# A hybrid decoder step on one Trainium2 core: x1 kept in the output and added by accumulating DMAs, the last tile's squares summed apart, and a GpSimd power in the first and the last norm

## The chip, the cores and the metric

The kernel runs on one core of one Trainium2 chip. The metric is the time of one execution on the device in microseconds (us), lower is better. The engines are TensorE (PE, with its weight loads as PEld), VectorE (DVE), ScalarE (ACT), GpSimd (POOL) and the DMA engines, whose transfers are issued here from the queue of SyncE (SP) and from that of GpSimd.

## What is computed

One layer of a hybrid decoder on 1024 prompt positions and 8 x 8 sample positions, 1088 columns in all, D = 1024, all in float32:

```python
h = rmsnorm(x, norm_mix_pre)
P = h @ w_in                      # ten blocks of 256 columns, for four mixers
mix = concat(conv(P), pool(P), hgrn2(P), conformer(P)) @ w_out
x = x + rmsnorm(mix, norm_mix_post)                     # "x1" below
h = rmsnorm(x, norm_ffn_pre)
ff = (silu(h @ w_gate) * (h @ w_up)) @ w_down           # hidden width 2816
x = x + rmsnorm(ff, norm_ffn_post)                      # yT, the output
# rmsnorm(x, g) = x * rsqrt(mean(x*x) + 1e-6) * g
```

The new states of the mixers are outputs too. Only `x1`, the two additions and the norms matter for the change.

## The kernel before

Features lie on the 128 partitions (eight tiles of 128 features), positions along the free dimension. Every product is made of three float32r products, of a high and a low part of each operand (`XH`, `XL`, `wop`), so each weight tile loaded from HBM is split by a cast on ScalarE and a subtraction on VectorE.

The work has four stages.

1. **Entry.** The rows of x come in position-major, nine tiles of 1024 features (`xs`), loaded from L204. For each of three chunks of positions (`CH`), `x_sq` (L214) squares the rows on ScalarE with a sum per row, `x_norm` (L222) makes the reciprocal root with `rsqrt_steps` (L102) and scales the rows, and `x_split` (L231) transposes them on TensorE and writes `XH` on ScalarE and `XL` on VectorE. `rsqrt_steps` is twelve small VectorE instructions: the mean plus epsilon, a first guess from the bits and the halved argument, and three Newton steps of three. The order on ScalarE, VectorE and TensorE is the one in which the code is written (the block from L240); GpSimd's and SyncE's is a scheduler's. Chunk 0 has two of the nine tiles.
2. **Mixers**, driven by hand-written queues of generators (`hook`, `fill`, L308 to L341).
3. **w_out, x1 and the gated product.** `residual` (L1142) adds the normed mix to x and stores the result, x1, in the HBM tensor `x1d` (L1155), half of the features for a piece of 272 positions at a time: eight stores. The gated products follow in Strassen form (L1388); their results go to HBM (`hd`, `hx`).
4. **w_down.** The first 16 hidden blocks are multiplied in Strassen form (L1616), into accumulators `acc[0..7]` (their tiles are called `t_...` and `acc`). The last six blocks are multiplied plainly by `down` (L1494, matmul at L1498), in three chunks of positions `DC` of 448, 384 and 256 columns. This last block of the program (L1729 to L1780) sets its own order on ScalarE, VectorE, TensorE and GpSimd. For each chunk c and each feature tile j it issues: the weight split of two tiles ahead (`ahead`), the load of x1 of this chunk if j is 0 (L1752 to L1756: four loads of two feature tiles), the products, the addition of the product to `acc[j]` on VectorE (L1761), the addition of the last square to the sum `sqa` (L1765), the square of `acc[j]` on ScalarE (L1767), for chunk 0 the additions of `add_p1` on GpSimd, and so many steps of the *previous* chunk's `finish` (L1770).

`finish` (L1713) closes a chunk: `stats` (L1077) sums `sqa` over the partitions with matmuls against a column of ones (L1082; a matmul on 128 positions stands twice in the counts of the trace), `rsqrt_steps` takes the root, `spread` transposes it over the partitions (L180), and for each of eight feature tiles VectorE scales `acc[j]` by gain and root (L1723), GpSimd (in the last chunk for j = 1, 4, 6, 7 VectorE) adds x1 (L1724), and SyncE stores the tile to `yT` (L1725). The chunks 0 and 1 are closed within the products of the chunks 1 and 2; the last chunk's closing stands alone at the end of the program. There the sum `sqa` takes the last square by one more addition on VectorE (L1773) ahead of `stats`.

SyncE's queue issues the loads of weights and the stores of `yT` in one order, and a store waits there for the addition that it stores.

## Time and profile before

| | |
|---|---|
| three runs | 1195.52 us median, 1193.73 to 1196.79 |
| the profiled execution | 1194.23 us, of which the span from the first to the last instruction is 1192.5 us |
| busy share of the span | PE 97%, DVE 75%, ACT 38%, POOL 8% |
| the chain that ended last | PE 85% of the span, DVE 5%, DMA 4% |
| DMA | 140.32 MB, mean 118 GB/s |

Busy times are averages over stages with different limits. PE is busy nearly all the time except at both ends of the program: the first matmul starts at 11.75 us, and after the last product, at 1175 us, only small matmuls follow. The view by stretches of time and the instructions in order of time show what each end waits for.

### The profile page before, as it was taken

To read this page: it belongs to the slowest core of one execution; us is meant where nothing else is said; L and a number is where in the kernel's file an instruction comes from. 1 tells how busy PE (TensorE), PEld (TensorE's weight loads), DVE (VectorE), ACT (ScalarE), POOL (GpSimd) and SP (SyncE) were. 2 spreads that over 40 slices of the span, in tenths; PEclk is the share of its full clock that TensorE was granted. 3 is DMA by queue.
4 is the path that set the end of the run, shared out by engine and by line. 5 is a ranking of instruction groups with operands and counts; after the bars stand their busy time and mean duration, and the time that the engine had idled before them with its cause. 6 is when DMAs were issued, how large, how long until landed. Compare 5 with 4: busy or idle time off the path is not lost.

```text
span 1192.5 us, 21885 instructions
## 1 busy us (share of the span) xinstructions
PE 1151.5 (97%) x8476; PEld 1116.0 (94%) x8476; DVE 892.2 (75%) x1853; ACT 456.3 (38%) x1006; POOL 100.4 (8%) x130
## 2 busy tenths in 40 slices
PE   5999999999999999999999999999999999999994
PEld 4899899998999999999999999999999999999994
DVE  6468979997675678777677787787676668887687
ACT  7534322253364453433333444344344442123321
POOL 1000000000000000000000000000001221036234
PEclk9999999999999999999999999999999999999997
DMA  8011112211155123031332453354364875654732
GB/s 261 29 43 24 36 37 68 41 36 36 33 161 169 39 74 129 23 103 69 105 103 83 159 168 113 127 176 146 98 196 130 280 261 168 239 165 126 258 109 89
DMA packets 105576, 140.32 MB, mean 118 GB/s; under 512 B 25152, under 2 KB 74432, under 8 KB 105472
## 3 DMA queue, kind: packets, MB, share of 16 engines
q1 hardware_dynamic: 99424, 115.52, 30.5%
q0 software_dynamic: 6048, 23.40, 5.6%
q8 instruction: 66, 1.08, 0.4%
q14 instruction: 38, 0.31, 0.1%
HBM read 98.31 MB, written 40.57 MB: 116 GB/s over the span
## 4 chain that ended last, share of the span: by engine, by line
PE 85%; DVE 5%; DMA 4%; issue 2%; ACT 2%; POOL 0%; SPq 0%; DVEq 0%; ACTq 0%; POOLq 0%
PE p L1388 27%; PE mm L984 18%; PE p L1616 13%; PE p L1116 8%; PE p L1297 6%; PE p L1498 4%; PE mm L139 2%; PE sm L798 2%; DMA hx<-hi 1%; DVE wop L65 1%; DMA hd<-hst 1%; DMA raw<-hx 1%; DVE xl L65 1%; DMA raw<-wgu 1%; PE p L1082 1%
## 5 line engine op out<-in xcount | busy, mean ns | idle before, releaser
L65 DVE TENSOR_TENSOR wop<-raw,wop 128x512 fp32r<-128x512 f32 (+2 forms) x296 | 197.9, 681 | 110.2 <-ACT wop L1007 100.3
L1007 ACT CAST wop<-raw 128x512 fp32r<-128x512 f32 (+1 forms) x240 | 142.5, 604 | 257.0 <-DVE raw L65 120.6
L1388 PE MATMUL p<-xh,wop 128*128 128x272 f32 x1216 | 235.3, 288 | 0.0
L1388 PEld LDWEIGHTS p<-xh,wop 128*128 128x128 f32 x1216 | 193.0, 188 | 0.0
L1388 PE MATMUL p<-t,wop 128*128 128x272 f32 x912 | 181.0, 290 | 5.7 <-DVE c L65 5.7
L984 PE MATMUL mm<-xh,wop 128*128 128x256 f32 (+2 forms) x864 | 176.8, 333 | 0.0
L1388 PE MATMUL p<-xl,wop 128*128 128x272 f32 x608 | 175.1, 288 | 0.0
L1388 PEld LDWEIGHTS p<-t,wop 128*128 128x128 f32 x912 | 147.3, 190 | 6.8 <-DVE c L65 6.8
L984 PEld LDWEIGHTS mm<-xh,wop 128*128 128x128 f32 x864 | 138.3, 188 | 6.2 <-issue 1.1
L1388 PE MATMUL p<-x,wop 128*128 128x272 f32 x456 | 132.5, 290 | 0.0
L1388 PEld LDWEIGHTS p<-xl,wop 128*128 128x128 f32 x608 | 114.3, 188 | 0.0
L1116 PE MATMUL p<-xh,wop 128*128 128x272 f32 x512 | 100.2, 292 | 2.0 <-DVE wop L65 2.0
L984 PE MATMUL mm<-xl,wop 128*128 128x256 f32 (+2 forms) x432 | 97.9, 335 | 0.0
L1388 PEld LDWEIGHTS p<-x,wop 128*128 128x128 f32 x456 | 86.5, 190 | 0.0
L1116 PEld LDWEIGHTS p<-xh,wop 128*128 128x128 f32 x512 | 82.1, 191 | 2.2 <-DVE wop L65 2.2
L1616 PE MATMUL p<-xh,wop 128*128 128x272 f32 x456 | 82.2, 289 | 1.1 <-ACT x L1627 1.1
L1616 PE MATMUL p<-xl,wop 128*128 128x272 f32 x456 | 81.4, 288 | 0.0
L71 DVE SCALAR_TENSOR_TENSOR y<-u,taps,y 128x1024 f32<-128x1024 f32 x60 | 77.0, 1284 | 1.6
L65 DVE TENSOR_TENSOR raw<-raw,raw 128x512 f32<-128x512 f32 (+1 forms) x123 | 71.3, 589 | 8.8 <-DMA raw<-wgu 7.3
L1116 PE MATMUL p<-xl,wop 128*128 128x272 f32 x256 | 74.3, 290 | 0.0
L1297 PE MATMUL p<-xh,wop 128*128 128x272 f32 x384 | 74.0, 289 | 0.0
L984 PEld LDWEIGHTS mm<-xl,wop 128*128 128x128 f32 x432 | 69.4, 188 | 3.4 <-issue 0.7
(332 smaller groups left out, 1988.1 us busy)
## 6 DMA issues: line engine op xcount, KB each, us to landing
raw<-wgu SPq DMA_DIRECT2D x88, 256.0 KB, 3.0
hx<-hi SPq DMA_DIRECT2D x84, 136.0 KB, 2.0
raw<-win SPq DMA_DIRECT2D x40, 256.0 KB, 3.0
hx<-x SPq DMA_DIRECT2D x64, 136.0 KB, 2.5
raw<-wdn SPq DMA_DIRECT2D x32, 256.0 KB, 3.7
xh<-hx POOLq DMA_DIRECT2D x15, 544.0 KB, 9.7
xl<-hx POOLq DMA_DIRECT2D x15, 544.0 KB, 10.5
x<-hx POOLq DMA_DIRECT2D x12, 544.0 KB, 9.3
```

What stands on the lines that cost most here:

```text
L65: (eng or V).tensor_tensor(out, a, b, op)
L71: (eng or V).scalar_tensor_tensor(out=out, in0=a, scalar=s, in1=b, op0=op0, op1=op1)
L139: PE.matmul(ps[c][:, :n], hl[:, wi, kk], X[k][:, o:o + n], start=k == 0 and wi == 0 and X is XH, stop=k == KT - 1 and wi == 1)
L798: PE.matmul(ps[:rows, g * P:(g + 1) * P], kk[:, o:o + rows], qz[hf][:, :, g * 64:(g + 1) * 64], start=True, stop=True, skip_group_check=True)
L984: PE.matmul(ps[c][:, :w], hl[:, wi, kk], X[k][:, o:o + w], start=k == order[0] and wi == 0 and X is XH, stop=k == order[-1] and wi == 1)
L1007: S.copy(hl[:, 0], raw)
L1082: PE.matmul(st[:, i:i + 1], sq[:, a:a + P], ones[:, :1], start=True, stop=True, skip_group_check=True)
L1116: PE.matmul(ps[nt][:, :PW], WO[nt][k // 4][:, wi, kk:kk + P], X[k][:, o:o + PW], start=k == korder[0] and wi == 0 and X is XH, stop=k == k ...
L1297: PE.matmul(ps[r][:, :PW], w[:, wi, (k % 4) * P:(k % 4 + 1) * P], X[k][:, o:o + PW], start=k == 0 and wi == 0 and X is XH, stop=k == KT - ...
L1388: PE.matmul(ps[:, :PW], wop[:, wi, kk * P:(kk + 1) * P], x(kk, xi), start=first and kk == 0 and wi == 0 and xi == 0, stop=kk == 3 and wi == 1,
L1498: PE.matmul(ps[:, :n], wd[:, wi, kk * P:(kk + 1) * P], hops[k][xi][:, o:o + n], start=first and kk == 0 and wi == 0 and xi == 0, stop=not ...
L1616: PE.matmul(ps[:, :PW], ws[name][wi][q], x[:, xi, pr], start=first and q == 0 and wi == 0 and xi == 0, stop=q == 1 and wi == 1, skip_group ...
```

## The change

- The HBM tensor `x1d` is gone. `residual` stores x1 in the output `yT` itself.
- In `finish` of chunk 0 and chunk 1, x1 is no longer loaded and added: after VectorE has scaled `acc[j]`, GpSimd's queue issues a DMA that adds the tile to what stands in `yT`. So eight loads of x1 (four of 448 KB, four of 384 KB), sixteen additions on GpSimd and sixteen stores from SyncE's queue go, and sixteen accumulating DMAs come. Chunk 2 still loads x1 (now from `yT`), adds and stores as before.
- In the last chunk the last square isn't added to `sqa`: `stats` runs on `sqa` without it, and a second `stats` adds the last square's sums in the same bank of PSUM.
- `rsqrt_pow` takes the place of `rsqrt_steps` in the first chunk's entry norm and in the last chunk's closing norm: the mean on VectorE, and one GpSimd instruction that raises it to the power -0.5.

```diff
+    mhalf = T(const, [P, 1], "mhalf")
+    V.memset(mhalf, -0.5)
...
+    def rsqrt_pow(src, shape, scale, tag):
+        m, y = T(const, shape, f"rs_{tag}m"), T(const, shape, f"rs_{tag}y")
+        TS(m, src, scale, EPS)
+        GP.tensor_tensor(y, m, mhalf[:, :1].to_broadcast(shape), ALU.pow)
+        return y
...
     def x_norm(c, ss):
-        for r in rsqrt_steps(ss[:, :len(idx)], [P, len(idx)], 1.0 / D, f"x{CH[c][1]}"):
-            yield
+        args = ss[:, :len(idx)], [P, len(idx)], 1.0 / D, f"x{CH[c][1]}"
+        if c == 0:
+            r = rsqrt_pow(*args)
+        else:
+            for r in rsqrt_steps(*args):
+                yield
...
-    def stats(sq, n):
+    def stats(sq, n, st=None, last=True):
-        st = bank()
+        first = st is None
+        if first:
+            st = bank()
-            PE.matmul(st[:, i:i + 1], sq[:, a:a + P], ones[:, :1], start=True, stop=True, skip_group_check=True)
+            PE.matmul(st[:, i:i + 1], sq[:, a:a + P], ones[:, :1], start=first and i == 0, stop=last, skip_group_check=True)
...
-    x1k = x1d.rearrange("(k p) t -> p k t", p=P)
+    x1k = yT.rearrange("(k p) t -> p k t", p=P)
...
-    def finish(c, sqa, x1t):
+    def finish(c, sqa, x1t, sq=None):
-        st, gr = stats(sqa, n)
-        for r in rsqrt_steps(st, [P, len(gr)], 1.0 / D, f"f{c}"):
+        st, gr = stats(sqa, n, last=sq is None)
+        if sq is not None:
             yield
+            stats(sq, n, st)
+        args = st[:, :len(gr)], [P, len(gr)], 1.0 / D, f"f{c}"
+        if x1t:
+            r = rsqrt_pow(*args)
+            yield
+        else:
+            for r in rsqrt_steps(*args):
+                yield
...
-            TT(y, y, x1t[j // 2][:, j % 2], ALU.add, eng=GP if c < 2 or j in (0, 2, 3, 5) else V)
-            SY.dma_start(yT[j * P:(j + 1) * P, o:o + n], y)
+            if x1t:
+                TT(y, y, x1t[j // 2][:, j % 2], ALU.add, eng=GP if j in (0, 2, 3, 5) else V)
+                SY.dma_start(yT[j * P:(j + 1) * P, o:o + n], y)
+            else:
+                GP.dma_start(yT[j * P:(j + 1) * P, o:o + n], y, accum_op=ALU.add)
...
-                for m in range(KT // 2):
+                for m in range(KT // 2 if c == 2 else 0):
...
             if j == KT - 1:
-                TT(sqa, sqa, sq, ALU.add)
-                prev, fin = fin, finish(c, sqa, x1[c])
-                if c == len(DC) - 1:
-                    next(fin)
+                if c < len(DC) - 1:
+                    TT(sqa, sqa, sq, ALU.add)
+                    prev, fin = fin, finish(c, sqa, x1[c])
+                else:
+                    prev, fin = fin, finish(c, sqa, x1[c], sq)
```

GpSimd's instructions at the end of the program, from the second half of chunk 1's closing to the last addition (`xl_...`, `xh_...` and `x_...` hold x1 there). Before:

```order
L65 TENSOR_TENSOR t_1_1352_10556<-t_1_1352_10556,xh_1685_13031 128x384
L65 TENSOR_TENSOR t_1_1353_10557<-t_1_1353_10557,xh_1685_13031 128x384
L65 TENSOR_TENSOR acc_1354_10558<-acc_1354_10558,xl_1686_13033 128x384
L65 TENSOR_TENSOR acc_1355_10559<-acc_1355_10559,xl_1686_13033 128x384
L65 TENSOR_TENSOR t_0_1348_10552<-t_0_1348_10552,xh_1717_13300 128x256
L65 TENSOR_TENSOR t_0_1350_10554<-t_0_1350_10554,xl_1718_13302 128x256
L65 TENSOR_TENSOR t_1_1351_10555<-t_1_1351_10555,xl_1718_13302 128x256
L65 TENSOR_TENSOR t_1_1353_10557<-t_1_1353_10557,x_13304 128x256
```

Now, the same place:

```order
L1751 DMA yT<-t_1_1351_10546 128x384
L1751 DMA yT<-t_1_1352_10547 128x384
L1751 DMA yT<-acc_1353_10548 128x384
L1751 DMA yT<-acc_1354_10549 128x384
L131 TENSOR_TENSOR rs_f2y_13519<-rs_f2m_13518,mhalf_78 128x2
L65 TENSOR_TENSOR t_0_1347_10542<-t_0_1347_10542,x_13266 128x256
L65 TENSOR_TENSOR t_0_1349_10544<-t_0_1349_10544,x_13268 128x256
L65 TENSOR_TENSOR t_1_1350_10545<-t_1_1350_10545,x_13268 128x256
L65 TENSOR_TENSOR t_1_1352_10547<-t_1_1352_10547,x_13270 128x256
```

The additions of chunk 1 have become DMA issues, and the power (L131) stands behind all of them and ahead of the last chunk's additions.

VectorE's instructions from the last product's addition to the first scaling of the last closing (`p_...` is a bank of PSUM, `xl_...` the sum of squares, `sq_...` a square, `rs_f2m` the mean). Before, the nine rows of the Newton steps cut after the first:

```order
L65 TENSOR_TENSOR acc_1355_10559<-p_13533,acc_1355_10559 128x256
L65 TENSOR_TENSOR xl_1635_12741<-xl_1635_12741,sq_12742 128x256
L65 TENSOR_TENSOR xl_1635_12741<-xl_1635_12741 128x256
L68 TENSOR_SCALAR rs_f2m_13559<-p_13556 128x2
L68 TENSOR_SCALAR rs_f2y_13561<-rs_f2m_13559 128x2
L68 TENSOR_SCALAR rs_f2h_13560<-rs_f2m_13559 128x2
L65 TENSOR_TENSOR rs_f2a_13562<-rs_f2y_13561 128x2
```

Now:

```order
L65 TENSOR_TENSOR acc_1354_10549<-p_13491,acc_1354_10549 128x256
L65 TENSOR_TENSOR xl_1634_12731<-xl_1634_12731,sq_12732 128x256
L68 TENSOR_SCALAR rs_f2m_13518<-p_13513 128x2
L71 SCALAR_TENSOR_TENSOR t_0_1347_10542<-t_0_1347_10542,prm_70,p_13522 128x256
L71 SCALAR_TENSOR_TENSOR t_0_1348_10543<-t_0_1348_10543,prm_70,p_13522 128x256
```

One addition and eleven small steps are gone between the product's addition and the first scaling; on TensorE the matmuls of L1082 for this chunk are four where they were two.

GpSimd's instructions at the start of the program (`y_...` is a row tile of x, `rs_...` a reciprocal root; the row ISA is a reload of a library of GpSimd's functions). Before:

```order
L454 MEMSET u_965 128x30
L454 MEMSET u_1678 128x30
L68 ISA
L68 TENSOR_SCALAR y_24_103<-y_24_103,rs_x384y_195 128x1024
L68 TENSOR_SCALAR y_27_106<-y_27_106,rs_x448y_279 128x1024
```

Now:

```order
L467 MEMSET u_955 128x30
L467 MEMSET u_1668 128x30
L131 ISA
L131 TENSOR_TENSOR rs_x256y_150<-rs_x256m_149,mhalf_78 128x2
L68 TENSOR_SCALAR y_25_105<-y_25_105,rs_x384y_185 128x1024
```

The reload keeps its place behind the last memset; the first instruction behind it is now the power of chunk 0's norm.

## Rows read from the trace of the kernel before

**Rows 1.** The page: TensorE's busy time, share of the span and instructions (its section 1), and the chain that ended last by engine (its section 4).

```profile
PE 1151.5 (97%) x8476; PEld 1116.0 (94%) x8476; DVE 892.2 (75%) x1853; ACT 456.3 (38%) x1006; POOL 100.4 (8%) x130
...
PE 85%; DVE 5%; DMA 4%; issue 2%; ACT 2%; POOL 0%; SPq 0%; DVEq 0%; ACTq 0%; POOLq 0%
```

**Rows 2.** Stretches of the program: from and to, length, then busy time (and instructions) of PE, PEld, DVE, ACT and POOL, granted clock, DMA share and GB/s. The first is everything from the end of the entry to the last chunk 0 product, the second chunk 1's products and chunk 2's first, the third a gap, the fourth chunk 2's other products, then the last norm, then the last closing.

```profile
41.00:1133.00 1092.00, 1082.48 (x8038) 1051.99 (x8036) 821.34 (x1674) 416.48 (x928) 69.31 (x95) 1.00 0.36 116
1133.00:1158.14 25.14, 25.14 (x153) 24.89 (x152) 20.41 (x41) 7.28 (x16) 10.59 (x8) 1.00 0.34 111
1158.14:1159.00 0.86, 0.05 (x1) 0.05 (x1) 0.76 (x3) 0.14 (x1) 0.00 (x0) 1.00 0.37 144
1159.00:1175.40 16.40, 16.34 (x135) 15.93 (x135) 14.27 (x36) 4.82 (x12) 6.53 (x6) 1.00 0.24 80
1175.40:1183.20 7.80, 1.70 (x6) 1.21 (x6) 5.53 (x18) 0.59 (x2) 2.61 (x3) 0.65 0.20 76
1183.20:1192.50 9.30, 0.00 (x0) 0.00 (x0) 5.91 (x12) 0.00 (x0) 2.85 (x4) 0.50 0.33 113
```

**Rows 3.** Instructions in order of time at the start: start, duration, engine, line, operation, output and inputs, and in brackets the idle time before it and what ended it.

```profile
4.07 0.18 POOL L454 MEMSET u<- 128x30 f32 x2
...
8.77 0.17 DVE L68 TENSOR_SCALAR rs_x256m<-ss 128x2 f32<-128x2 f32 x1 [4.30 <-ACT h L219]
...
10.94 1.42 DVE L68 TENSOR_SCALAR y<-y,rs_x256y 128x1024 f32<-128x1024 f32 x2
...
11.75 0.48 PE L236 MATMUL sm<-cst,y 128*128 128x128 f32 x1 [11.75 <-DVE y L68]
...
12.47 0.18 ACT L219 ACTIVATION_READ_ACCUMULATOR h<-y 128x1 f32 x1
...
12.92 0.47 ACT L237 ACTIVATE xh<-sm,prm 128x256 fp32r<-128x256 f32 x1 [0.27 <-PE sm L236]
...
18.80 1.60 POOL L68 TENSOR_SCALAR y<-y,rs_x384y 128x1024 f32<-128x1024 f32 x1 [14.55 <-DVE rs_x384y L71]
```

**Rows 4.** TensorE in order of time around the gap at 1158 us, columns as in rows 3, and the matmuls of chunk 1's spread.

```profile
1157.86 0.28 PE L1498 MATMUL p<-xl,wop 128*128 128x256 f32 x1
1158.95 0.83 PE L1082 MATMUL p<-ones,sq 128*128 128x1 f32 x6 [0.81 <-DVE sq L65]
...
1162.00 0.54 PE L180 MATMUL p<-cst,rs_f1y 128*128 128x128 f32 x3
```

**Rows 5.** VectorE in order of time ahead of that gap: the weight split, the addition of the last product of chunk 1, and the last two additions of squares.

```profile
1155.61 1.18 DVE L65 TENSOR_TENSOR wop<-raw,wop 128x384 fp32r<-128x384 f32 x1
1156.72 0.55 DVE L65 TENSOR_TENSOR acc<-p,acc 128x384 f32<-128x384 f32 x1
1157.19 1.71 DVE L65 TENSOR_TENSOR sq<-sq,xl 128x384 f32<-128x384 f32 x2
```

**Rows 6.** All engines in order of time from the last product to the last addition.

```profile
1174.99 1.17 DVE L65 TENSOR_TENSOR xl<-xl 128x256 f32<-128x256 f32 x1
1175.06 0.28 PE L1498 MATMUL p<-xl,wop 128*128 128x256 f32 x1
...
1176.09 1.12 DVE L71 SCALAR_TENSOR_TENSOR acc<-acc,prm,p 128x384 f32<-128x384 f32 x2
1176.82 2.12 POOL L65 TENSOR_TENSOR acc<-acc,xl 128x384 f32<-128x384 f32 x2 [0.94 <-POOL t L65]
1177.13 0.41 DVE L65 TENSOR_TENSOR acc<-p,acc 128x256 f32<-128x256 f32 x1
...
1177.64 0.42 ACT L1767 ACTIVATE xl<-acc 128x256 f32<-128x256 f32 x1 [2.06 <-DVE acc L65]
...
1178.20 1.03 DVE L65 TENSOR_TENSOR xl<-xl 128x256 f32<-128x256 f32 x1
...
1179.28 1.01 PE L1082 MATMUL p<-ones,xl 128*128 128x1 f32 x4 [3.94 <-DVE xl L65]
1180.33 0.16 DVE L68 TENSOR_SCALAR rs_f2m<-p 128x2 f32<-128x2 f32 x1 [1.10 <-PE p L1082]
...
1182.51 0.69 PE L180 MATMUL p<-cst,rs_f2y 128*128 128x128 f32 x2 [2.22 <-DVE rs_f2y L71]
1183.24 0.87 DVE L71 SCALAR_TENSOR_TENSOR t<-t,prm,p 128x256 f32<-128x256 f32 x2 [0.78 <-PE p L180]
```

**Rows 7.** VectorE's weight splits of 384 columns from 1119 to 1141.3 us, while GpSimd does nothing: count, busy time, mean ns of one.

```profile
L65 DVE TENSOR_TENSOR wop<-raw,wop 128x384 fp32r<-128x384 f32 x9 | 4.8, 556 | 3.4 <-ACT wop L1007 3.4
```

**Rows 8.** The same instruction from 1144 to 1159 us, while GpSimd adds x1.

```profile
L65 DVE TENSOR_TENSOR wop<-raw,wop 128x384 fp32r<-128x384 f32 x5 | 4.6, 917 | 0.0
```

**Rows 9.** Groups of GpSimd's instructions over the whole run: count, busy time, mean ns of one, idle time before them.

```profile
L1541 POOL DMA_DIRECT2D xh<-hx x15 | 8.1, 539 | 4.3 <-PE p L1616 1.6 <-DMA xl<-hx 1.4 <-DVE wop L65 0.5
...
L65 POOL TENSOR_TENSOR t<-t,x 128x256 f32<-128x256 f32 x1 | 0.7, 722 | 0.8 <-DVE t L71 0.8
...
L596 POOL MEMSET u<- 128x8 f32 x2 | 0.2, 118 | 0.0
```

**Rows 10.** Granted clock of TensorE after the last product (columns as in rows 2).

```profile
1176.40:1177.40 1.00, 0.00 (x0) 0.00 (x0) 1.00 (x3) 0.00 (x0) 0.58 (x1) 1.00 0.54 197
1177.40:1178.40 1.00, 0.00 (x0) 0.00 (x0) 0.90 (x3) 0.42 (x1) 1.00 (x2) 0.64 0.00 0
```

**Rows 11.** DMA issues by tile over the whole run: queue, count, KB each, median us from issue to landing.

```profile
xh<-hx POOLq DMA_DIRECT2D x15, 544.0 KB, 9.7
...
yT<-t SPq DMA_DIRECT2D x6, 224.0 KB, 1.9
```

More of the change, by code (lines that the diff above doesn't have):

```diff
@@ L53, in body @@
 def body(ctx, tc, xn, xT, win, wout, wgu, wdn, par, con, msk, poolw, s_conv, s_pool, s_hgrn, s_conf,
-         yT, o_conv_p, o_pool_p, o_hgrn_p, o_conf_p, o_conv_s, o_pool_s, o_hgrn_s, o_conf_s, x1d, hd, hx):
+         yT, o_conv_p, o_pool_p, o_hgrn_p, o_conf_p, o_conv_s, o_pool_s, o_hgrn_s, o_conf_s, hd, hx):
     nc = tc.nc
@@ L1076, in body @@
     LAG = 2
-    def stats(sq, n):
+    def stats(sq, n, st=None, last=True):
         gr = [min(a, n - P) for a in range(0, n, P)]
-        st = bank()
+        first = st is None
+        if first:
+            st = bank()
         for i, a in enumerate(gr):
-            PE.matmul(st[:, i:i + 1], sq[:, a:a + P], ones[:, :1], start=True, stop=True, skip_group_check=True)
-        return st[:, :len(gr)], gr
+            PE.matmul(st[:, i:i + 1], sq[:, a:a + P], ones[:, :1], start=first and i == 0, stop=last, skip_group_check=True)
+        return st, gr
     def spread(r, gr):
@@ L1133, in norm @@
         yield None
-        for r in rsqrt_steps(st, [P, len(gr)], 1.0 / D, tag):
+        for r in rsqrt_steps(st[:, :len(gr)], [P, len(gr)], 1.0 / D, tag):
             yield -0.2
@@ L1804 @@
          ("conf_p", (2, P, 30)), ("conv_s", (2, P, 8, 2)), ("pool_s", (2, P, 8, 15)), ("hgrn_s", (2, P, 8, 64)),
-         ("conf_s", (2, P, 8, 30)), ("x1", (D, NT)), ("hd", (NF, P, NT)), ("hx", (NPAIR, 7, P, 4 * PW))]
+         ("conf_s", (2, P, 8, 30)), ("hd", (NF, P, NT)), ("hx", (NPAIR, 7, P, 4 * PW))]
 def kernel(**inputs):
```

## The prediction

> **What bounds the kernel now.** I read the page first. TensorE is busy 97% of the span and carries 85% of the chain that ended last [rows 1], so only time in which TensorE stands still can be won without changing its work, and the change leaves its work alone. Next I read the busy times by stretches [rows 2]: from 41 to 1133 us TensorE is busy 1082 of 1092 us, and nothing that the change touches waits there but stores of x1, which go to another tensor of the same size. The change can act in three places only: the entry, until the first matmul at 11.75 us [rows 3]; a gap of 0.8 us at 1158 us, in front of chunk 1's sum of squares [rows 4]; and the end, where TensorE has finished its last product at 1175.3 us and the program goes on for 17 us. The instructions in order of time at these places show what each waits for.
>
> At the end [rows 6] the last matmul of a product starts at 1175.06 and takes 0.28 us. Its addition to `acc` on VectorE starts only at 1177.13, 1.8 us later, since VectorE is still at an addition of squares that took 1.17 us and at two scalings of chunk 1's closing. Then come the square on ScalarE (1177.64), the last addition of squares (1178.20, 1.03 us), the matmuls against ones (1179.28, 1.01 us), twelve small VectorE steps (1180.33 to 1182.5), the spread (0.69 us) and the first scaling at 1183.24. From the end of the product to that scaling it is 7.9 us, and the last closing takes the other 9.3 us [rows 2].
>
> Why VectorE is late is seen by comparing one instruction in two stretches: the weight split of 384 columns takes 556 ns while GpSimd is idle [rows 7] and 917 ns on the mean while GpSimd adds x1 [rows 8]. VectorE and GpSimd hold each other up.
>
> **The change part by part.**
>
> *Chunk 0 and 1: additions become DMAs.* Sixteen GpSimd additions of over 1 us each go; each is replaced by a DMA issue from GpSimd's queue, 539 ns by the issues that it has already [rows 9]. The freed time on GpSimd is worth nothing itself. What counts is that VectorE works at its undisturbed speed. Ahead of the gap the split took 1.18 us, and the last two additions of squares 1.71 us together [rows 5]; undisturbed, the addition to `acc` for the last product of chunk 1, which ends at 1156.0, starts there instead of at 1156.72, and the last sum is ready by about 1157.8. TensorE wants it when chunk 2's first product is through, at 1158.14, so the gap closes: **0.8 us**, and no less than 0.4 if half the disturbance stays.
>
> The same holds in chunk 2. A step with two scalings has a split of 0.5, an addition of 0.35, one of squares of 0.35 and 1.1 us for the scalings, 2.3 us, against TensorE's 2.1 us for a step (16.4 us for seven products and 1.2 of small matmuls [rows 2, 4]; the first of the eight is ahead of the gap). VectorE falls behind by a few tenths in two steps, and the step with a single scaling and the later ones without a split give it back. I count VectorE as idle when the last product ends.
>
> SyncE's queue loses the stores that waited for GpSimd, so weight loads come no later than before. Eight loads of x1 go too; TensorE waited for none, and that is worth nothing. GpSimd's queue gets a new order: the last power stands behind the sixteen DMA issues. The last two scalings of chunk 1 end before the last product does, so two issues of 0.54 us are over before the mean is ready. This cover is gone if the issue takes several times as long.
>
> *The last sum.* Counted from the end of the last product, 1175.34, on the old clock: the addition 0.06 later and 0.41 long, 1175.8; the square on ScalarE 0.1 later and 0.42 long, 1176.3. Meanwhile VectorE adds the square before it (0.42 undisturbed), and TensorE's first four matmuls run from 1176.2. Eight of them are due. Before, six took 0.83 us at chunk 1's end [rows 4] and four took 1.01 us at the end [rows 6]; by then the granted clock had fallen to its lower level, from 1.00 at 1177.4 to 0.5 [rows 10], 2.3 us after the products ended. In the changed order the pause is 0.9 us, so I take the faster row: 1.1 us, to 1177.3. At the lower clock it would be 2.0.
>
> *The power.* The mean, 0.16 us and a step between engines of 0.04 to 0.1 on each side: 1177.6. GpSimd's power of 128x2 has no row. Below, it can't be faster than the memset of eight columns, 0.12 us [rows 9]; above, I take the 1.6 us of the 128x1024 scaling [rows 3], though a power is more than a product per element and could exceed that. The nearest row is the smallest addition with two inputs, 128x256 in 0.72 us [rows 9], and two columns are far fewer: I take 0.4 us. Then 1178.0. The spread takes 0.36 at the full clock (two of the three that took 0.54 [rows 4]), and the first scaling starts at 1178.45 instead of 1183.24: **4.8 us**, between 2.5 (power 1.6, lower clock) and 5.1.
>
> *The last closing* has the same instructions: eight scalings, four additions on each engine, eight stores. Nothing.
>
> *The entry.* The power replaces the steps from 8.94 to 10.94 us [rows 3]: with 0.4 us and the steps between engines the rows are scaled from 9.5 us on, 1.4 us earlier, and so is the first matmul. But ScalarE's `xh`, which the first product needs, stood at 12.92 us with a wait of only 0.27 us; ahead of it ScalarE squares the rows of chunk 1, until 12.65 [rows 3]. So 0.27 us is won there, and more only where TensorE's earlier start makes it quicker behind that. **0.3 us**, between -0.5 (power at 2 us) and 1.4.
>
> Here a rule speaks against it. GpSimd's queue holds a library reload between its last memset, which ends at 4.25, and its first computing instruction, which starts at 18.80 [rows 3]. The trace shows no record of it, only that 14.5 us were enough. Before, nothing wanted GpSimd until 18.6; now the power does at 9.0. If the reload were over by 9.0, the term is 0.3. The Trainium skill (GPSIMD Engine Reference, 2.1 Instruction dispatch) says that the first call of freshly loaded code costs about 6 us; by that the power starts at about 10.2, an estimate from that page, the rows are scaled near the old time, the term is 0.1 and the sum 5.7. No run so far shows it.
>
> **Sum.** 0.3 + 0.8 + 4.8 = 5.9 us. The profiled execution took 1194.23 us, 1.3 below the median of 1195.52; taken off the median, that gives **1189.6 us**.
>
> **The rivals.**
>
> *The power is slow, or VectorE stays disturbed.* GpSimd now writes descriptors instead of adding, and that may hold VectorE too; a power of 2 to 3 us makes the closing term 2 to 3 and the entry -0.5 to -1.2. For it: the power has no row. Against it: GpSimd's 539 ns issues are short. It gives 2 to 3.5 us, 1192 to 1193.5.
>
> *The reload ends late.* If it lasts nearly until GpSimd's first instruction did, 18.8 us, the rows are scaled 8 us later, and all behind shifts: 5.6 won, 8 lost, 1198. It decides from a reload that ends after 15 us. Against it: the rows would not show a first scaling by GpSimd at 18.80 that follows VectorE's last step so closely unless the reload was done before.
>
> *The accumulating DMAs set the end.* This one ends slower. A plain store of 224 KB lands 1.9 us after its issue [rows 11]. An accumulation reads and writes; if it took 3.8 us and one could only follow another, sixteen of them from 1142 us on would end at 1203 us, 10.5 us behind the old end: 1206. It decides from 3.2 us each (50 us for sixteen). If they overlap, the last, issued near 1174, has 12 us until the new end at 1186.6, more than the 9.7 us that GpSimd's DMAs of 544 KB take in their bursts [rows 11]. For it: nothing in the trace accumulates. Against it: that queue's DMAs overlap, and these are smaller.
>
> *It doesn't do what it says.* The additions go for certain, by the order of instructions; but VectorE could be late at the last product for its own work alone (scalings and squares), 2.3 against 2.1 us a step. Then 1 to 1.5 us of the closing's 4.8 stay: 1191.
>
> **How the numbers follow.** A difference of 0.3% (3.6 us) is about what a measurement of this kernel can tell from none. The forecast has 55%; with the last rival, still mostly faster, 12%; more than 7 us won because the entry gains its whole 1.4 us, 6%; the slow power or disturbance 15%, nearly all of it within 0.3%; the late reload 7%, within 0.3% or beyond; the accumulations 5%. So faster 0.74, same 0.19, slower 0.07. The range takes the forecast's bounds: 8.0 us won at best gives 1187.5, less half a microsecond for the median's scatter, 1187.0; 2.5 us won gives 1193.0. Outside lie the two rivals of the other side and some of the slow power.
>
> **What would show it.** Right: no TensorE gap in front of chunk 1's sum of squares; VectorE's split at 0.56 us throughout; the last addition to `acc` within 0.2 us of the last product; under 4 us from the last product to the first scaling; the power near 0.4 us. Wrong: GpSimd's first power far behind the first mean; issues of accumulating DMAs well over 0.54 us, or their landing after the last store; TensorE's last small matmuls at the lower clock. If the power takes over 2 us, or the program ends on an accumulation, the forecast is wrong.

## The result, and the profile after

| | before | changed |
|---|---|---|
| first comparison, median (lowest to highest) | 1194.62 us (1192.17 to 1196.79) | 1181.66 us (1180.14 to 1182.58) |
| ratio, 95% interval | | 0.9893, 0.9868 to 0.9919 |
| second comparison (e1 below) | 1194.88 us | 1187.30 us, 0.9929, 0.9906 to 0.9953 |
| profiled execution, span | 1192.5 us | 1180.8 us |

The direction was as forecast, the size was not: 5.9 us were predicted, the first comparison gave 13.0 and the second 7.6. The page of the changed kernel, its head and the chain that ended last (they answer to [rows 1]):

```profile
span 1180.8 us, 21827 instructions
...
PE 1145.0 (97%) x8480; PEld 1111.1 (94%) x8480; DVE 881.4 (75%) x1831; ACT 455.5 (39%) x1006; POOL 96.8 (8%) x132
...
PE 84%; DVE 5%; DMA 4%; issue 2%; ACT 2%; POOL 1%; SPq 0%; DVEq 0%; ACTq 0%; POOLq 0%
```

TensorE's busy time is the first surprise. It has four instructions more than before by this count (the second set of sums at the end is two matmuls, and each stands twice) and is busy 6.5 us less.

The entry in order of time (the answer to [rows 3]):

```profile
8.58 0.17 DVE L68 TENSOR_SCALAR rs_x256m<-ss 128x2 f32<-128x2 f32 x1 [4.56 <-ACT h L228]
...
8.83 0.71 POOL L131 TENSOR_TENSOR rs_x256y<-rs_x256m,mhalf 128x2 f32<-128x2 f32 x1 [4.55 <-DVE rs_x256m L68]
9.57 1.42 DVE L68 TENSOR_SCALAR y<-y,rs_x256y 128x1024 f32<-128x1024 f32 x2 [0.82 <-POOL rs_x256y L131]
...
10.38 0.47 PE L249 MATMUL sm<-cst,y 128*128 128x128 f32 x1 [10.38 <-DVE y L68]
...
12.48 0.46 ACT L250 ACTIVATE xh<-sm,prm 128x256 fp32r<-128x256 f32 x1
...
12.99 0.58 PE L148 MATMUL mm<-xh,wop 128*128 128x256 f32 x1 [0.61 <-ACT xh L250]
```

The power starts 0.08 us behind the mean and takes 0.71. From the mean to the first matmul it is 1.80 us instead of 2.98. But ScalarE's `xh` is hardly earlier, and from the mean to the 151st matmul, at 41 us, it is 32.3 us against 32.6.

The gap of [rows 4] in front of chunk 1's sum of squares is closed; VectorE has the sum ready before TensorE is through with the product:

```profile
1150.09 0.56 DVE L65 TENSOR_TENSOR sq<-sq,xl 128x384 f32<-128x384 f32 x1 [0.19 <-ACT xl L1793]
...
1150.56 0.28 PE L1513 MATMUL p<-xl,wop 128*128 128x256 f32 x1
...
1150.71 0.83 PE L1097 MATMUL p<-ones,sq 128*128 128x1 f32 x6
```

The end, from the last product on (to be laid beside [rows 6]):

```profile
1166.59 0.28 PE L1513 MATMUL p<-xl,wop 128*128 128x256 f32 x1
1166.67 1.73 POOL L1751 DMA_DIRECT2D yT<-acc  x2 [1.06 <-DVE acc L71]
1166.90 0.43 DVE L65 TENSOR_TENSOR acc<-p,acc 128x256 f32<-128x256 f32 x1 [0.23 <-PE p L1513]
1167.24 0.42 DVE L65 TENSOR_TENSOR xl<-xl,sq 128x256 f32<-128x256 f32 x1
1167.42 0.42 ACT L1793 ACTIVATE xl<-acc 128x256 f32<-128x256 f32 x1 [1.62 <-DVE acc L65]
1167.72 1.05 PE L1097 MATMUL p<-ones,xl 128*128 128x1 f32 x8 [0.85 <-DVE xl L65]
1168.81 0.16 DVE L68 TENSOR_SCALAR rs_f2m<-p 128x2 f32<-128x2 f32 x1 [1.15 <-PE p L1097]
1169.05 0.72 POOL L131 TENSOR_TENSOR rs_f2y<-rs_f2m,mhalf 128x2 f32<-128x2 f32 x1 [0.65 <-DVE rs_f2m L68]
1169.82 0.43 PE L189 MATMUL p<-cst,rs_f2y 128*128 128x128 f32 x2 [1.06 <-POOL rs_f2y L131]
1170.30 0.87 DVE L71 SCALAR_TENSOR_TENSOR t<-t,prm,p 128x256 f32<-128x256 f32 x2 [1.33 <-PE p L189]
```

The last product's end is 1166.87. The addition to `acc` follows 0.03 us later (before, 1.8), and the first scaling 3.43 us later (before, 7.90). VectorE's weight split is undisturbed through both closings, and GpSimd's queue pays more for an issue than before (VectorE's group from 1130 to 1168 us, GpSimd's two groups over the whole run; [rows 7 to 9]):

```profile
L65 DVE TENSOR_TENSOR wop<-raw,wop 128x384 fp32r<-128x384 f32 x12 | 6.7, 555 | 2.0 <-ACT wop L1020 2.0
```

```profile
L1751 POOL DMA_DIRECT2D yT<-t x12 | 10.4, 948 | 46.9 <-DVE t L71 46.4 <-issue 0.5
L1751 POOL DMA_DIRECT2D yT<-acc x4 | 3.5, 1024 | 3.3 <-issue 2.3 <-DVE acc L71 1.1
```

An accumulation of 224 KB lands 5.2 us after its issue, by the list of DMA issues; the plain store took 1.9 [rows 11].

Where did 11.7 us of span go? Matmuls of the two traces were paired in order, and the distances from one matmul's start to the next one's compared. After 41 us some 8,280 of these distances differ by less than 20 ns; their differences add up to **-5.3 us**. The larger ones add up to -2.6: the gap (-0.9) and one fall of TensorE's clock less than before (-1.7), while the waits for VectorE elsewhere cancel out. The closing gives -4.5, the entry and its loads -0.5. And the stretch from the first scaling to the end of the span is *longer*: 10.52 us against 9.22, though from the first scaling to VectorE's last addition it is 6.05 us in both.

### The profile page after: what moved, and what is told of

Its sections match the earlier page's. It is cut to its first block, busy times and chain, and to the rows that moved or that the text cites. A ratio compares the mean times of both kernels' runs of the same rounds, so it can differ in the third digit from the quotient of the medians.

```text
span 1180.8 us, 21827 instructions
## 1 busy us (share of the span) xinstructions
PE 1145.0 (97%) x8480; PEld 1111.1 (94%) x8480; DVE 881.4 (75%) x1831; ACT 455.5 (39%) x1006; POOL 96.8 (8%) x132
## 4 chain that ended last, share of the span: by engine, by line
PE 84%; DVE 5%; DMA 4%; issue 2%; ACT 2%; POOL 1%; SPq 0%; DVEq 0%; ACTq 0%; POOLq 0%
PE p L1403 27%; PE mm L997 16%; PE p L1631 14%; PE p L1131 8%; PE p L1513 6%; PE p L1312 5%; PE mm L148 2%; PE sm L811 1%; DVE wop L65 1%; DMA raw<-wgu 1%; DMA hx<-hi 1%; DVE raw L65 1%; DMA y<-xn 1%; DMA raw<-hx 1%; PE sm L886 1%
## 5 line engine op out<-in xcount | busy, mean ns | idle before, releaser
L1403 PE MATMUL p<-xh,wop 128*128 128x272 f32 x1216 | 235.1, 288 | 0.0
L1403 PEld LDWEIGHTS p<-xh,wop 128*128 128x128 f32 x1216 | 193.3, 188 | 0.0
L1403 PE MATMUL p<-t,wop 128*128 128x272 f32 x912 | 179.3, 288 | 5.2 <-DVE c L65 5.2
L1403 PE MATMUL p<-xl,wop 128*128 128x272 f32 x608 | 175.6, 289 | 0.0
L997 PE MATMUL mm<-xh,wop 128*128 128x256 f32 (+2 forms) x864 | 175.3, 331 | 0.0
L1403 PEld LDWEIGHTS p<-t,wop 128*128 128x128 f32 x912 | 145.6, 188 | 6.5 <-DVE c L65 6.5
L997 PEld LDWEIGHTS mm<-xh,wop 128*128 128x128 f32 x864 | 137.4, 188 | 6.0 <-issue 1.1
L1403 PE MATMUL p<-x,wop 128*128 128x272 f32 x456 | 131.0, 287 | 0.0
L1403 PEld LDWEIGHTS p<-xl,wop 128*128 128x128 f32 x608 | 114.4, 188 | 0.0
L997 PE MATMUL mm<-xl,wop 128*128 128x256 f32 (+2 forms) x432 | 97.3, 333 | 0.0
L1403 PEld LDWEIGHTS p<-x,wop 128*128 128x128 f32 x456 | 86.0, 189 | 0.0
L1631 PE MATMUL p<-xh,wop 128*128 128x272 f32 x456 | 81.6, 287 | 1.1 <-ACT x L1642 1.1
L1631 PE MATMUL p<-xl,wop 128*128 128x272 f32 x456 | 81.0, 287 | 0.0
L997 PEld LDWEIGHTS mm<-xl,wop 128*128 128x128 f32 x432 | 69.2, 188 | 3.3 <-issue 0.8
```

Of the source, the lines that this page charges most:

```text
L997: PE.matmul(ps[c][:, :w], hl[:, wi, kk], X[k][:, o:o + w], start=k == order[0] and wi == 0 and X is XH, stop=k == order[-1] and wi == 1)
L1403: PE.matmul(ps[:, :PW], wop[:, wi, kk * P:(kk + 1) * P], x(kk, xi), start=first and kk == 0 and wi == 0 and xi == 0, stop=kk == 3 and wi == 1,
L1631: PE.matmul(ps[:, :PW], ws[name][wi][q], x[:, xi, pr], start=first and q == 0 and wi == 0 and xi == 0, stop=q == 1 and wi == 1, skip_group ...
```

## Experiments

Three things were not in the prediction: the shorter matmuls in a stretch that the change doesn't edit, the longer last stretch, and an entry that gained nothing. The theory for the first: the change makes the pool `const` smaller by 96 bytes (four small tiles less for the root, one more for the exponent, of 32 bytes each). `const` and the pools of `xh`, `xl` and `x` are allocated from the same side of SBUF, so all these tiles lie 96 bytes higher. In the built programs the first xh tile stands at byte 156000 of a partition before and at 156096 after; weights and PSUM places of all matmuls in L997, L1403 and L1631 are the same. Rival: chance between executions. Of e6 and e8 to e12 below there is one execution each; they are read by their rows, not by their times.

**e1: the changed kernel again.**

> The changed kernel once more, unaltered, as the yardstick for the next three on the same chip. Between 41 and 1133 us, where the change edits nothing, its profiled execution was 6 to 7 us shorter than that of the kernel before. Theory A (addresses): `const` shrank by 96 bytes, so every tile allocated on the same side (xh, xl, x) moved from an address 32 past a multiple of 64 to a multiple of 64, and matmuls that read them are about 1% shorter; a fixed property of the build. Theory B (scatter): the two profiled executions differ by chance in that stretch. A: ratio to the kernel before 0.989 again, matmuls of L1631 in 930 to 1095 us every 124.5 ns again. B: ratio nearer 0.995, and these spacings anywhere between 124.5 and 125.6.

1187.30 us (six runs, 1181.13 to 1191.86), 0.9929. The spacings came again to 0.05 ns (L997 on xh 165.7, L1631 on xh 124.4), so they belong to the build. The runs scatter for another reason: the profiled one, 1190.1 us of span, has four falls of the clock to 1.2 GHz between 300 and 960 us where the first profile has one. In the stretch with the first of them TensorE was busy all the time in both profiles, yet the clock was granted differently (busy times by stretch, columns as in [rows 2]; of e1, then of the first profile of the same kernel):

```profile
300.00:320.00 20.00, 20.00 (x109) 17.67 (x108) 10.76 (x39) 3.89 (x6) 0.00 (x0) 0.83 0.17 40
```

```profile
300.00:320.00 20.00, 20.00 (x131) 17.96 (x130) 12.71 (x43) 5.83 (x10) 0.00 (x0) 1.00 0.16 40
```

22 matmuls less in 20 us. The other three falls come behind waits of TensorE. In the 7.4 us ahead of the one at 901.4 us it was busy for 4.45 us; in the first profile it stood still there nearly as long, and the clock stayed (e1, then the first profile):

```profile
894.00:901.40 7.40, 4.45 (x36) 4.23 (x34) 6.54 (x13) 4.42 (x9) 0.00 (x0) 1.00 0.34 106
```

```profile
894.00:901.40 7.40, 4.84 (x39) 4.69 (x38) 6.79 (x16) 1.76 (x3) 0.00 (x0) 1.00 0.50 159
```

Before the last closing, e1's profile has 13.7 us more at 1.2 GHz. Half of that, 6.8 us, is an estimate of what it costs, of the 9.3 us by which its span is longer; another 1.2 us is its first mean, which comes at 9.82 us instead of 8.58. The mean granted clock of the first comparison's four runs was 0.993 to 0.996, that of these six 0.989 to 0.994. So the clock helped the 13.0 us and hurt the 7.6; whether by chance alone or by the chip on which they ran, no run here separates.

**e2 and e3: an unused tile of 32 bytes in `const`**, in the changed kernel and in the kernel before.

```diff
+    T(const, [P, 8], "pad")
```

> The changed kernel with an unused tile of 32 bytes in `const`, so that xh, xl and x lie 32 past a multiple of 64 again. A: 3 to 5 us slower than the changed kernel on this chip, matmuls on x, xh and xl in 41 to 340 us and 930 to 1095 us 1 to 2 ns longer each. B: within 1 us of it.

> The kernel before with the same unused tile of 32 bytes, so that xh, xl and x lie at multiples of 64; nothing else differs. A: 3 to 5 us faster than the kernel before (about 1190). B: the same time (ratio 1.000, within 0.1%).

e2: 1188.85 us, 1.5 slower than e1, less than expected and within the scatter of e1's runs. e3: 1192.69 us, 0.9981 of the kernel before (0.9966 to 0.9996), 2.2 us faster: an unused tile alone changes the time. But the multiple of 64 is not the rule: e3's matmuls on xh in L985 (L997 in the changed kernel) fell from 167.7 to 166.7 ns, those of 930 to 1095 us stayed at 125.6, where e2's also were. The theory was right on addresses and wrong on which.

**e4: the kernel before again.**

> The kernel before, unaltered, for a second profile of it. A: spacings of L1616's matmuls 125.6 ns as in the first profile. B: they differ from the first profile by as much as the changed kernel's did (1 ns). The wait of 1.85 us at 705 us and the fall of the clock at 901 us, which only the first profile of the kernel before has, come again if they belong to it, and not if they are chance.

1193.80 us, 0.9992. All spacings as in its first profile (167.7, 125.6). Two matmuls at 705 us that start 1.85 us apart in the first profile start 0.60 us apart here, so that wait is chance. The fall of the clock at 901 us is not: it came again, at 898 us. The 17 profiles of both kernels and their variants have their falls at the same places of the program, at 305 to 309 us in 9 of them, at 337 to 342 us in 10, at 895 to 903 us in 15. The changed kernel's first profile is one of the two without the last; e1, the same kernel, has it. So the 1.7 us of one fall less above are the luck of that execution.

**e5: the kernel before at the changed kernel's addresses.**

```diff
-            return T(const, shape, f"rs_{tag}{i}", dt)
+            return T(const, [P, 4], f"rs_{tag}{i}", dt)[:, :shape[1]] if tag == "f" else T(const, shape, f"rs_{tag}{i}", dt)
...
-        for r in rsqrt_steps(st, [P, len(gr)], 1.0 / D, f"f{c}"):
+        for r in rsqrt_steps(st, [P, len(gr)], 1.0 / D, "f"):
...
+    T(const, [P, 40], "pad")
```

> The kernel before with const smaller by 96 bytes (the three closings' small tiles share buffers, and an unused tile of 160 bytes fills up), so that xh, xl and x lie at exactly the changed kernel's addresses; nothing else of the change. Absolute address as the cause: matmuls of 41 to 340 us on xh 165.7 ns apart (kernel before 167.7), those of 930 to 1095 us 124.4 (125.6), and 3.5 to 5 us faster than the kernel before. Rival, another part of the build (the x1 tensor that is gone, the number of instructions): spacings as with the tile of 32 bytes, 166.7 and 125.6, and 2 us faster at most.

1190.61 us against 1194.33, 0.9973 (0.9955 to 0.9991): 3.7 us for nothing but addresses. Paired with the first profile of the kernel before, its small differences add up to -5.3 us, the same as the changed kernel's; e4, the kernel before against itself, gives +0.2. One view shows it: matmuls of the Strassen w_down product in 130 us without a gap (busy times by stretch, of that line alone: PE and its count, PEld and its count, granted clock, DMA share, GB/s). Before, changed, e5:

```profile
950.00:1080.00 130.00, 130.00 (x1038) 130.00 (x1037) 1.00 0.60 202
```

```profile
950.00:1080.00 130.00, 130.00 (x1047) 130.00 (x1046) 1.00 0.61 204
```

```profile
950.00:1080.00 130.00, 130.00 (x1047) 130.00 (x1046) 1.00 0.61 203
```

**e13: the whole change at the old addresses.**

```diff
+    T(const, [P, 24], "pad")
```

> The whole change, with an unused tile of 96 bytes in const, so that xh, xl and x lie at the addresses of the kernel before. If address and edits are the whole of the gain: the end and the gap as in the changed kernel, matmuls of 930 to 1095 us 125.6 ns apart as in the kernel before, and 4.1 us (2.5 to 5.5) faster than the kernel before. Rival, the edits also act in the middle of the program in a way not found yet: 7 us or more.

1189.36 us against 1194.61, 0.9967 (0.9953 to 0.9982): 3.9 us by the ratio, 5.3 by the two medians. The same view:

```profile
950.00:1080.00 130.00, 130.00 (x1037) 130.00 (x1037) 1.00 0.60 201
```

Its closing takes 3.43 us, the last stretch 10.52, as in the changed kernel. So the edits are worth 4 to 5 us and the addresses about as much: 3.7 by e5's medians, 5.3 by the paired traces.

**e7 and e8: the additions back on GpSimd**, for both chunks (e7, whose edit follows) and for chunk 1 alone (e8, with `c in (1, 2)` in the first line).

```diff
-                for m in range(KT // 2 if c == 2 else 0):
+                for m in range(KT // 2 if c in (0, 1, 2) else 0):
...
-        if x1t:
+        if c == 2:
             r = rsqrt_pow(*args)
...
-                TT(y, y, x1t[j // 2][:, j % 2], ALU.add, eng=GP if j in (0, 2, 3, 5) else V)
+                TT(y, y, x1t[j // 2][:, j % 2], ALU.add, eng=GP if c < 2 or j in (0, 2, 3, 5) else V)
```

> The changed kernel with chunk 0's and 1's additions on GpSimd and plain stores again (x1 still kept in yT, loaded from there). GpSimd's additions delay VectorE: the gap ahead of chunk 1's sum of squares is back at 0.8 to 1.1 us, and from the last product's end to the first scaling it is 4.5 to 5.2 us instead of 3.4. Rival, VectorE is late for its own work: gap and 3.4 us stay as in the changed kernel. GpSimd's last drain, which ended 1.2 us behind everything else in the changed kernel: it is 3.5 us long from GpSimd's last addition, as before, with 42 DMAs on its queue instead of 58. In all 1 to 2 us slower than the changed kernel.

> The changed kernel with only chunk 0 by accumulating DMAs, chunk 1 by GpSimd additions and plain stores. GpSimd's queue then has 50 DMAs, the last accumulation over long before the end. If its closing drain takes a fixed time for each DMA that its queue had (3.53 us for 42, 4.83 for 58, so 83 ns each), it is 4.2 us. If it waits for late accumulations, it is 3.5. The gap ahead of chunk 1's sum of squares stays closed, as chunk 0's closing runs under chunk 1's products; the last stretch is like that of the kernel with all additions back, 4.5 to 5.2 us.

e7: 1188.75 us, 0.996 (0.9943 to 0.9977). TensorE's wait in front of chunk 1's sum is back, 0.9 us. From the last product's end (1170.81) to the first scaling it is 5.73 us instead of 3.43. In e8 the gap stays closed and the closing takes 5.72: chunk 0's additions make the gap, chunk 1's make VectorE late at the end. e7 in order of time:

```profile
1170.22 0.41 DVE L65 TENSOR_TENSOR acc<-p,acc 128x256 f32<-128x256 f32 x1
...
1170.44 1.00 POOL L65 TENSOR_TENSOR t<-t,xh 128x384 f32<-128x384 f32 x1 [0.95 <-DVE t L71]
...
1170.56 1.17 DVE L65 TENSOR_TENSOR xl<-xl 128x256 f32<-128x256 f32 x1
...
1171.65 1.13 DVE L71 SCALAR_TENSOR_TENSOR acc<-acc,prm,p 128x384 f32<-128x384 f32 x2
...
1172.70 0.41 DVE L65 TENSOR_TENSOR acc<-p,acc 128x256 f32<-128x256 f32 x1
```

An addition of squares that takes 0.42 us alone takes 1.17 while GpSimd adds. The Trainium skill (SBUF — State Buffer, Who interferes with whom) says that a VectorE instruction with two SBUF inputs and a GpSimd instruction that reads SBUF lock each other out; these rows agree.

The two kernels also settle the longer last stretch. GpSimd's queue ends with a drain, which starts under its last addition. The rows of the closing line for that queue (count, shortest, median and longest in ns, first and last start in us), before, changed, and e8:

```profile
L1846 POOLq DRAIN  x3: 40/102/4279, 1187.4 to 1192.2; - x3
```

```profile
L1873 POOLq DRAIN  x3: 40/93/5586, 1174.5 to 1180.5; - x3
```

```profile
L1873 POOLq DRAIN  x3: 40/102/4932, 1175.8 to 1181.3; - x3
```

Counted from the end of GpSimd's last addition the drain lasts 3.52 us with 42 DMAs issued from that queue (before, e3, e4, e5, e7), 4.17 with 50 (e8) and 4.83 with 58 (changed, e1, e2): 84, 83 and 83 ns for each DMA of the whole program, however long ago: in e8 the last accumulation had landed at 1154.1 us, 22 us before the drain began. Before, it ended with SyncE's own last waits, 0.2 us behind them; in the changed kernel 1.5 us behind. The Trainium skill (VectorE: DVE Perf Modes, The DRAIN you can't avoid) counts drains that every kernel has at about 12 ns each; GpSimd's last one here was 300 to 400 times that.

**e6: VectorE's steps in the first norm again** (`rsqrt_steps` for every chunk; two of the closings share buffers and an unused tile keeps the addresses).

> The changed kernel with VectorE's steps instead of GpSimd's power in the first norm (addresses of xh, xl and x kept). First matmul 1.2 us later, at 11.6; but ScalarE's xh at the same 12.5 to 12.9, so that by 41 us it is only 0.2 to 0.5 us behind the changed kernel, whose entry term this is. Rival, the entry is worth its whole 1.4 us: 1.2 us or more behind at 41 us.

The first matmul is 2.98 us behind the mean instead of 1.80, and at the 151st matmul it is 32.24 us: in the eight profiles with the power and the same addresses it was 31.95 to 32.66. The entry's power is worth nothing that can be seen.

**e12: ScalarE's first two xh tiles ahead of its two squares.**

```diff
-        next(sq[1])
-        ss1 = next(sq[1])
         x_split(0, 0)
         x_split(0, 1)
         next(sq[1])
+        ss1 = next(sq[1])
+        next(sq[1])
```

> The changed kernel with ScalarE's first two xh tiles ahead of its two squares of chunk 1's rows, behind which they stood until 12.48 us though the first matmul began at 10.38. If ScalarE's order kept the entry from gaining, xh starts under 0.6 us after the first matmul's end, the first product's matmul 1.0 to 1.8 us earlier against the first matmul than in the changed kernel (2.6 us behind it there), and 0.5 to 1.5 us of it are left at 41 us. Rival, the rows of chunk 1 are late for it and take it back: nothing left at 41 us.

The first product's matmul is 3.50 us behind the mean instead of 4.41, so ScalarE's order did hold it. But at the 151st matmul it is 33.19 us, 0.9 worse than the changed kernel, so nothing is left, as the rival had it. What took it back shows at the third xh tile: three squares of chunk 1's rows in a row now stand ahead of it on ScalarE, and TensorE waits for it, where it didn't in the changed kernel:

```profile
16.50 0.58 PE L148 MATMUL mm<-xh,wop 128*128 128x256 f32 x1 [1.06 <-ACT xh L250]
```

That chunk 1's rows would also be late for TensorE, as the rival says, is not shown.

**e9 and e10: VectorE's steps in the last norm; the last squares added before the sum.** Each undoes one edit of the closing (in e9 unused bytes keep the addresses).

```diff
...
-        if x1t:
-            r = rsqrt_pow(*args)
-            yield
-        else:
-            for r in rsqrt_steps(*args):
-                yield
+        for r in rsqrt_steps(*args):
+            yield
```

```diff
-                if c < len(DC) - 1:
-                    TT(sqa, sqa, sq, ALU.add)
-                    prev, fin = fin, finish(c, sqa, x1[c])
-                else:
-                    prev, fin = fin, finish(c, sqa, x1[c], sq)
+                TT(sqa, sqa, sq, ALU.add)
+                prev, fin = fin, finish(c, sqa, x1[c])
```

> The changed kernel with VectorE's steps in place of GpSimd's power in the last closing (addresses of xh, xl and x kept). From the mean to the spread the kernel before took 2.2 us for its steps, the changed one 1.0 for mean, power and the ways between. From the last product's end to the first scaling: 4.6 us instead of 3.4, and 4.9 if the clock falls in the longer pause and the spread is slower for it. Rival, the power gains nothing, since the clock and the small matmuls set the time: 3.4 to 3.7 us.

> The changed kernel with the last tile's squares added on VectorE and one set of small matmuls instead of two (power kept). In the changed kernel eight small matmuls took 1.05 us from the moment at which VectorE was done with the squares before, and the last square was ready 0.2 us after that. Joint: an addition of 0.42 us behind the last square, then four matmuls of 0.5 us. From the last product's end to the first scaling 3.4 to 3.6 us, so the split of the squares is worth 0.2 at most. Rival, the split is worth what the prediction took it for (an addition of squares off the path): 3.8 us or more.

e9: 4.59 us from the last product's end to the first scaling, so the power is worth 1.16. e10: 3.88, more than expected:

```profile
1175.79 0.42 DVE L65 TENSOR_TENSOR xl<-xl 128x256 f32<-128x256 f32 x1 [0.21 <-ACT xl L1793]
1176.27 0.60 PE L1097 MATMUL p<-ones,xl 128*128 128x1 f32 x4 [1.49 <-DVE xl L65]
...
1177.93 0.69 PE L189 MATMUL p<-cst,rs_f2y 128*128 128x128 f32 x2 [1.06 <-POOL rs_f2y L131]
```

The addition and four matmuls cost 0.2 us more than eight matmuls, and the spread, at 0.69 instead of 0.43, another 0.26: by then the clock had fallen to 1.2 GHz, at 1177.1, 2.3 us after the last product. But that fall can't be put down to the undone split. In e6 and e12, which have the changed kernel's closing with its eight matmuls, the clock also fell before the spread, 2.7 and 2.6 us after the last product, and their first scaling comes at 3.68 us. The spread of e6:

```profile
1173.22 0.69 PE L190 MATMUL p<-cst,rs_f2y 128*128 128x128 f32 x2 [1.06 <-POOL rs_f2y L132]
```

At the same clock, then, it is 3.88 against 3.68: the split of the squares is worth 0.2 us, as expected, and the rival's 3.8 is reached by the clock alone.

**e11 and e14: three of the last closing's additions on GpSimd**, not four. Both are the same kernel; e14 is its timing.

```diff
-                TT(y, y, x1t[j // 2][:, j % 2], ALU.add, eng=GP if j in (0, 2, 3, 5) else V)
+                TT(y, y, x1t[j // 2][:, j % 2], ALU.add, eng=GP if j in (0, 2, 3) else V)
```

> The changed kernel with three of the last closing's additions on GpSimd (tiles 0, 2 and 3) instead of four, the last of which was tile 5. GpSimd's drain, 4.83 us behind its last addition with 58 DMAs on its queue, begins 1.4 us earlier; VectorE has one addition of 0.43 us more. From the first scaling to the end of the span: 9.6 to 9.8 us instead of 10.5, and the stores' landing now ends the program. Rival, the drain ends at a fixed distance behind the last store or the last accumulation: 10.5 us or more.

> The changed kernel with three of the last closing's additions on GpSimd instead of four, as in e11_early_pool, timed. By the traces 1.2 us faster than the changed kernel: 8.5 to 9 us faster than the kernel before, where the changed kernel was 7.6 on a chip and 13.0 on another. Rival, the falls of the clock cover it: no more than the changed kernel's 7.6.

From the first scaling to the end 9.24 us instead of 10.52, better than expected, since VectorE, alone at the end, needs only 0.23 us more for the added addition. e14: 1181.56 us against 1194.61, **0.9898** (0.9878 to 0.9918), 12 to 13 us faster than the kernel before and, by the last stretch, 1.3 faster than the changed one. The drain now ends 0.2 us ahead of SyncE's last waits, so the stores set the end again.

**e15: e14 at another address** (`T(const, [P, 16], "pad")`).

> e14_best with an unused tile of 64 bytes in const: xh, xl and x 64 bytes lower, 32 above those of the kernel before. If only multiples of 64 mattered, the spacings are those of the changed kernel (124.4 ns in 930 to 1095 us). By the four addresses seen (125.6, 125.6, 125.6 and 124.4) the changed kernel's was the lucky one: 125 to 126, and 2 to 4 us slower than e14_best.

1187.70 us, 0.9941 (0.9919 to 0.9964). L1632's matmuls on xh came every 125.0 ns and the mixers' on xh every 167.4, where the kernel before had 125.6 and 167.7, though the tiles lie at multiples of 64: 6.1 us slower than e14 for 64 unused bytes, more than the 2 to 4 expected, and 5.3 by the paired traces. The changed kernel's address was the best of five.

## Why the prediction was wrong, step by step

- **The step that failed** is the first one: "the change leaves its work alone", so that from 41 to 1133 us only stores to another tensor of the same size were seen. The change edits nothing there, but it resizes `const`, and half a per cent of the time of 8,000 matmuls is 5.3 us by the paired traces (e5, timed: 3.7), nearly as much as the whole forecast. It could have been read ahead: the diff adds one tile to `const` and leaves out four (the halved argument and the product of the steps, in two norms), and the pools of the moving operands stand behind it. What a shift does could not be read from one trace.
- **The gap, 0.8:** right, 0.9, for the reason given (e8: chunk 0's additions).
- **The closing, 4.8:** right in mechanism and nearly in size, 4.47. VectorE was idle when the last product ended, the eight matmuls took 1.05 us for 1.1 forecast, at the full clock. That the spread too ran at the full clock was in part luck: in three of the nine profiles with this closing (e6, e11, e12) the clock had fallen before it was through, and the first scaling came 0.14 to 0.25 us later. The power took 0.72 us, not 0.4: the nearest row of [rows 9], 0.72 for 256 columns, was the right price, and scaling it down by columns was the error. Undone one at a time: additions 2.3, power 1.2, split 0.2.
- **The last closing, nothing:** wrong by 1.3. Its instructions did stay the same to 0.01 us; what follows them was left out of the sum. The rival in which the accumulating DMAs set the end named the right cause and the wrong place: the last had landed at 1172.1 us, 8.7 before the end, but each added 83 ns to GpSimd's drain.
- **The entry, 0.3:** 0.0 (e6). The prediction saw that ScalarE's `xh` held it back, but took what was left for a gain.
- **The reload of GpSimd's library:** its rival fell. The power began 0.08 us after the mean at 8.83 us, where the Trainium skill's 6 us for a first call (GPSIMD Engine Reference, 2.1 Instruction dispatch), counted from 4.25, would by an estimate have put it at 10.2. No run here shows when the reload took place.
- **The issue of an accumulating DMA:** 0.95 to 1.02 us instead of 0.54. It stayed hidden, since the last two issues were over at 1168.40 and the mean at 1168.97.

Edits by the traces 0.9 + 4.5 + 0.0 - 1.3 = 4.1, measured alone 3.9 by the ratio (e13). With 5.3 for the addresses it makes 9.4, between the two comparisons' 13.0 and 7.6 and 0.3 below the first one's interval. The first profile adds 1.7 for the fall of the clock that it lacks and 0.5 for its entry: 11.6 of the 11.7 us of span. Open is why the clock falls in one execution and not in the next at the same place of the program: it moves a run by several us, and whether the changed kernel's falls are fewer for a reason of its own was not settled.

## What to carry to other kernels

When a change resizes a small pool, compare the addresses of the matmuls' moving operands in the two builds before the traces, and give a version with an unused tile that restores them: otherwise a shift is taken for the edit's own gain, or hides it. Count the DMAs on GpSimd's queue as time at the end of the program, and let GpSimd finish early. An engine taken off a short path helps most through what it stops disturbing: the additions moved away were worth twice the power.

## What the runs showed of the hardware

- The start of a matmul's moving operand changed its pace. With 272 columns the mean spacing in 930 to 1095 us was 125.6 ns with the first xh tile at 155968, 156000 and 156064, 125.0 at 156032 and 124.4 at 156096. The Trainium skill (SBUF — State Buffer, Door 1: The DMA port swizzle) speaks of lines of 16 bytes. By lines alone these starts, all multiples of 32, should be alike; measured, they are not. One stretch doesn't tell the whole: over all matmuls, against the kernel before at 156000, the small differences add up to -2.3 us at 155968, -0.2 at 156032, -3.1 at 156064 and -5.3 at 156096 (0.2 is the scatter of such a sum, by e4). No run here shows which bits of the address decide, nor whether it is the start itself or its place beside the weights, which kept their addresses.
- GpSimd's closing drain took 83 ns for each DMA that its queue had issued in the program: 3.52 us for 42, 4.17 for 50, 4.83 for 58. The 8 and 16 that were added are accumulations; that plain ones count alike rests on the 42, which are all plain.
- TensorE's clock fell at the same places of the program in most of the 17 profiles, at 895 to 903 us in 15. Three of the four falls in e1 come behind waits: TensorE was busy for 5.64 of the 7.6 us ahead of the one at 341.6, for 4.45 of 7.4 ahead of 901.4, for 4.50 of 7.2 ahead of 949.2. Whether the clock falls behind such a wait differs between executions of one program.
- A GpSimd power of 128x2 took 0.71 to 0.72 us, as long as an addition of 128x256 (0.72).
- An accumulating DMA cost GpSimd's queue 0.95 to 1.02 us to issue, a plain one 0.55, and landed after 5.2 us for 224 KB, a plain store from SyncE's queue after 1.9.
